# Up stage of two feed-forward blocks: block work of the head on VectorE alone, five gate tiles ahead

## The chip, the cores and the metric

The kernel runs on one core of a Trainium2 chip (trn2). The core has TensorE (PE in the profile, its weight loads PEld), VectorE (DVE), ScalarE (ACT), GpSimd (POOL) and SyncE (SP), which issues most of the transfers. Each engine runs its own list of instructions in order; semaphores tie the lists together. The metric is the device time of one execution in microseconds, the median of three runs: 2109.07 us for the kernel before.

## The reference

One layer of an encoder over 1040 rows (1024 and 16 meta rows) of 1024 features:

```python
h = h + 0.5 * swiglu(rmsnorm(h, ffn1_norm[l]), ffn1_w_gate[l], ffn1_w_up[l], ffn1_w_down[l])
u = rmsnorm(h, mix_norm[l]);  z = u @ w_in[l]
...  # differential attention (4 heads) and windowed attention (8 heads), both into w_out
h = h + jnp.concatenate([out_a, out_b], axis=-1) @ w_out[l]
h = h + 0.5 * swiglu(rmsnorm(h, ffn2_norm[l]), ffn2_w_gate[l], ffn2_w_up[l], ffn2_w_down[l])
h = rmsnorm(h, final_norm);  return h[:, N_META:]

def swiglu(x, w_gate, w_up, w_down):
    return (jax.nn.silu(x @ w_gate) * (x @ w_up)) @ w_down
```

The hidden width of a SwiGLU is 2816, that is 22 tiles of 128. All is float32. The change touches the normed input and the gate and up products of both SwiGLU blocks.

## The kernel before

**Stages.** In order: the up stage of the first SwiGLU (`ffn_up`, 1040 columns in two halves of H = 520), its down stage, the projections, both attentions, the output product, the up stage of the second SwiGLU (1024 columns, H = 512), its down stage and the last norm. A matrix product of float32 numbers is made of three passes: each operand is split into a rounded part (`hi`, a cast on ScalarE, line 117) and the rest (`lo`, a subtraction, line 114), and `product` (line 226) adds hi x hi, hi x lo and lo x hi.

**The up stage.** The normed input is cut in four blocks: feature half 1 or 2 by column half a or b. `b11` and `b21` are the two feature halves of column half a, `b22` the second feature half of column half b. Gate and up products of all 22 tiles are made by a Strassen-like scheme from seven block operands: `b11`, `b21`, `b22` and the differences `t1` to `t4`. Per tile there are seven products, each of four 128-row steps times three passes; where H is 520 each pass is two matmuls of 260 columns (24 matmuls a product), where H is 512 one (12 matmuls a product). Two of the seven (`lead_a` with `b11`, `lead_b` with `b21`) need column half a alone and can be made ahead of the rest; their weights go through tiles `rg0` (raw, two buffers), `wah` and `wal` (hi and lo, three buffers). The other five need `t2`, `t1`, `t3`, `b22` and `t4`, in that order in a tile, with weight sums `s1`, `s2`, `s4` made on GpSimd.

**The head.** "Head 1" is the start of the program, up to the point where products follow each other without a break; "head 2" is the same place in the second up stage. In it `prepare` loads or makes column halves a and b (tiles `ha`, `hc` and `hb`, `hd`) and norms half a (`first_half`, 16 pieces of work: norm, line 149, and split), and `combine` does half b (`second_half`): norms, differences, splits. `eng()` there deals the subtractions out to VectorE and GpSimd by prices of 0.61 and 1.24. `prepare1` sums the squares for the norm by additions on VectorE, `combine1` by additions on VectorE and GpSimd; a product with `ones` (line 650) sums over the partitions. Between the pieces of `second_half` four gate tiles (`LEAD = 4`) are interleaved, at its yields.

**The order of the work.** The program is written in this order, and a scheduler then places each instruction in the list of its engine by a timeline that it reckons; so an engine's list is not the order of the text. A list is kept on the chip: an instruction that waits holds up all behind it on its engine.

Of the kernel before, what the change touches and what calls it, by code (L numbers as in the profile page):

```python
# [34 lines left out]
OFF = 248  # L35
LEAD = 4
G_BUFS = 3
# [14 lines left out]
def layer(  # L52
# [137 lines left out]
    def ffn_up(H, wg, wu, nlead, prepare, combine, accs):  # L190
# [5 lines left out]
        with ExitStack() as st:  # L196
# [40 lines left out]

            ahead = {}

            def lead_a(f, src):  # L240
# [12 lines left out]

            def lead(f):
                def src(i):
                    t = la3.tile([P, hw], F32, tag="rg0", name="rg0", bufs=2)
                    nc.sync.dma_start(t, wg[f][:, i * hw : (i + 1) * hw])
                    return t

                lead_a(f, src)  # L260
                lead_b(f, src)

            with ExitStack() as st_r:
                lr = Rings(st_r, "lr", "right")
                for tag, bufs in (
                    ("nsq", 2), ("ns", 1), ("nr", 1), *((n, 1) for n in accs), ("ha", hk), ("hb", hk), ("x2", hk), ("hc", hk), ("hd", hk),
                ):
# [5 lines left out]
                la3 = Rings(st, "la3").reserve("rg0", 2).reserve("wah", 3).reserve("wal", 3)  # L273
# [8 lines left out]
            for tag, bufs in (  # L282
                ("rg0", 1), ("ru0", 1), ("s", 3), ("wbh", 2), ("wbl", 2), ("rg1", 1), ("ru1", 1),
                ("u2", 1), ("m5", 1), ("u3", 1), ("wch", 3), ("wcl", 3), ("ge", 1), ("gt", 1), ("g", G_BUFS),
            ):
                la4.reserve(tag, bufs)
# [9 lines left out]
            for f in range(FT):  # L296
# [6 lines left out]
                def s_tile():  # L303
                    return la4.tile([P, hw], F32, tag="s", name="s", bufs=3)
# [9 lines left out]
                product(p2, weight(la4, "wb", s2, 2), "t2", True)  # L314
                if nxt is not None:
# [4 lines left out]
                p3, p3f = ps_tile("p3")  # L320
                product(p3, weight(la4, "wb", s1, 2), "t1", True)
                tt(gp, a21, a11, a21, ALU.subtract)
# [14 lines left out]

                g2 = tmp(la5, "ge" if paired and not odd else "g", G_BUFS)
                tt(gp, u3, u3, m5, ALU.add)
# [16 lines left out]
                if not paired:  # L356
                    nc.gpsimd.dma_start(g_d[f][:, :H], g1)
                elif odd:
                    put("b21", g1)
                    tt(nc.vector, t2, g1, t2, ALU.subtract)  # L360
                    put("t4", t2)
                else:
                    put("b11", g1)
                    t1 = tmp(la5, "gt")
# [12 lines left out]
    def second_half(firsts, hts, gi, r, blk, pool, H):  # L377
        hk = KT // 2
        load = {nc.vector: 0.0, nc.gpsimd: 0.0}
        price = {nc.vector: 0.61, nc.gpsimd: 1.24}  # L380

        def eng():
            e = min(load, key=lambda e: load[e] + price[e])
            load[e] += price[e]
            return e

        def parts(n, j, src):
            hi, lo = (t[:, j, :] for t in blk[n])
            split(hi, lo, src, eng())

        x2 = {}
# [12 lines left out]
        yield  # L404
        for j in range(hk):
            tt(eng(), hts[j], hts[j + hk], hts[j], ALU.subtract)
            parts("t3", j, hts[j])
        for j in range(hk):
            parts("b22", j, hts[j + hk])
        for j in range(hk):  # L410
            b21 = firsts[j + hk]
            tt(eng(), b21, b21, x2[j], ALU.subtract)
            parts("t4", j, b21)

# [216 lines left out]

    E1, E2 = ([nc.vector if c == "v" else nc.gpsimd for c in e] for e in ("vv", "vp"))

    def rstd_pair(srcs, n, width, pool, subs, full, engs):

        half = len(srcs) // 2
        accs = []
        for c, eng in enumerate(engs):
            acc = pool.tile([P, 520], F32, tag=f"nacc{c}", name="nacc")[:, :n]
            for i, s in enumerate(srcs[c::2]):  # L640
                if i == 0:
                    nc.scalar.activation(acc, s, AF.Square)
                else:
                    sq = pool.tile([P, 520], F32, tag="nsq", name="nsq")[:, :n]
                    nc.scalar.activation(sq, s, AF.Square)
                    tt(eng, acc, acc, sq, ALU.add)
            accs.append(acc)
        for c, acc in enumerate(accs):
            for o, (c0, cn) in subs:
                nc.tensor.matmul(o, ones, acc[:, c0 : c0 + cn], start=c == 0, stop=c == len(accs) - 1)  # L650
        return newton(n, width, pool, full)

    def prepare1(pool, psum, blk, ps_tile, subs):
# [15 lines left out]
    def combine1(state, pool, blk, ps_tile, subs):  # L669
        H = L // 2  # L670
        a, b = state
        outs, full = ps_tile("p2")
        r = rstd_pair(b, H, D, pool, list(zip(outs, subs)), full, E2)
        yield
        yield from second_half(a, b, 0, r, blk, pool, H)
# [600 lines left out]
    def combine2(halves, pool, blk, ps_tile, subs):  # L1276
# [3 lines left out]
        r = rstd(b, H, D, pool, list(zip(outs, subs)), full)  # L1280
        yield
        yield from second_half(a, b, 2, r, blk, pool, H)
# [115 lines left out]
```

## Time and profile before

| what | value |
|---|---|
| median of 3 runs | 2109.07 us (2106.53 to 2112.87) |
| profiled execution, its own time | 2112.15 us |
| its span | 2110.4 us |
| PE busy | 1947.8 us, 92% of the span |
| PEld, DVE, ACT, POOL busy | 1695.8, 1304.6, 877.2, 1042.0 us |
| share of the chain that ended last: PE, DVE, DMA | 70%, 11%, 6% |

The profiled execution is 1.75 us longer than its span (work around the span), and 3.1 us above the median. TensorE is busy for most of the span; the chain that ended last runs over it. Where it is idle is read stage by stage. PEclk is the clock granted to TensorE, 1.00 for 2.4 GHz and 0.50 for 1.2 GHz.

### The profile page before, as it was taken

What the parts mean: (1) busy time and instruction counts of PE and PEld (TensorE: products, weight loads), DVE (VectorE), ACT (ScalarE), POOL (GpSimd) and SP (SyncE); (2) the same over time, 40 slices, a digit from 0 to 9 for tenths busy, and PEclk for the clock granted to TensorE, in tenths of its full rate; (3) what the DMA queues carried; (4) which work ended last, traced back from release to release, by engine and by line L of the source; (5) the groups of instructions that cost most, each with busy time, mean ns of one, the idle gap of its engine ahead of it and who ended that gap; (6) DMA issues with size and microseconds to landing.
All of it is one profiled execution on the core that took longest, in us unless ns stands there. A gap on an engine that the chain in (4) does not pass through costs nothing.

```text
span 2110.4 us, 30362 instructions
## 1 busy us (share of the span) xinstructions
PE 1947.8 (92%) x11484; PEld 1695.8 (80%) x11484; DVE 1304.6 (62%) x1804; ACT 877.2 (42%) x1609; POOL 1042.0 (49%) x856
## 2 busy tenths in 40 slices
PE   4799999998999999899977999877999999989998
PEld 4799999998999889777755777665788888867877
DVE  7865555547865572276667777478555555488745
ACT  5333333334532441266557666343333333344433
POOL 5655545444543651476457433036655545455453
PEclk9899999999999999999989999998999999999999
DMA  3232232327431452444442321522422332284222
GB/s 134 90 121 88 96 116 83 105 85 289 159 114 33 160 161 76 126 132 122 98 122 63 102 87 54 161 80 70 140 105 79 116 105 90 105 313 162 74 80 80
DMA packets 104563, 241.52 MB, mean 114 GB/s; under 512 B 14048, under 2 KB 28848, under 8 KB 104416
## 3 DMA queue, kind: packets, MB, share of 16 engines
q1 hardware_dynamic: 92896, 201.91, 30.3%
q0 software_dynamic: 11520, 37.67, 4.6%
q8 instruction: 90, 1.47, 0.3%
q14 instruction: 57, 0.47, 0.1%
HBM read 167.23 MB, written 65.44 MB: 110 GB/s over the span
## 4 chain that ended last, share of the span: by engine, by line
PE 70%; DVE 11%; DMA 6%; ACT 5%; POOL 3%; issue 3%; SPq 1%; DVEq 0%; POOLq 0%; ACTq 0%
PE p L226 37%; PE pA L557 8%; PE pC L557 4%; PE pj L167 4%; PE pv L867 3%; PE pd L167 2%; PE do L1166 2%; PE pB L557 2%; PE ds L763 2%; PE po L167 1%; DVE bl L114 1%; PE do L167 1%; PE wo L1000 1%; ACT dp L769 1%; PE wt L989 1%
## 5 line engine op out<-in xcount | busy, mean ns | idle before, releaser
L226 PE MATMUL p<-b_hi,wal 128*128 128x260 f32 (+1 forms) x528 | 146.5, 333 | 26.9 <-DVE wal L114 26.9
L226 PE MATMUL p<-b_hi,wah 128*128 128x260 f32 (+1 forms) x528 | 147.8, 334 | 13.2 <-ACT m L244 9.8
L226 PE MATMUL p<-b_lo,wah 128*128 128x260 f32 (+1 forms) x528 | 145.6, 331 | 7.7 <-DVE b_lo L114 7.7
L226 PE MATMUL p<-t_hi,wch 128*128 128x260 f32 (+1 forms) x528 | 140.5, 320 | 3.6 <-DVE u L114 3.6
L226 PE MATMUL p<-t_lo,wbh 128*128 128x260 f32 (+1 forms) x528 | 142.6, 320 | 0.0
L226 PE MATMUL p<-t_hi,wbh 128*128 128x260 f32 (+1 forms) x528 | 140.0, 321 | 1.5 <-ACT wbh L117 1.5
L226 PE MATMUL p<-t_lo,wch 128*128 128x260 f32 (+1 forms) x528 | 140.4, 320 | 0.0
L226 PE MATMUL p<-t_hi,wcl 128*128 128x260 f32 (+1 forms) x528 | 139.9, 319 | 0.0
L226 PE MATMUL p<-t_hi,wbl 128*128 128x260 f32 (+1 forms) x528 | 139.9, 320 | 0.0
L114 DVE TENSOR_TENSOR u<-p,m 128x520 f32<-128x520 f32 (+1 forms) x88 | 61.0, 693 | 111.2 <-PE p L226 107.4
L226 PEld LDWEIGHTS p<-b_hi,wal 128*128 128x128 f32 x528 | 92.2, 199 | 36.7 <-DVE wal L114 28.7
L117 ACT CAST wbh<-s 128x512 fp32r<-128x512 f32 x88 | 54.6, 621 | 156.2 <-PE p L226 149.4
L114 DVE TENSOR_TENSOR wal<-rg,wah 128x512 fp32r<-128x512 f32 x88 | 81.0, 922 | 61.9 <-ACT wah L117 61.8
L557 PE MATMUL pA<-bl,wh 128*128 128x260 f32 (+1 forms) x432 | 115.6, 322 | 1.6 <-DVE bl L114 1.6
L557 PE MATMUL pA<-bh,wh 128*128 128x260 f32 (+1 forms) x432 | 116.0, 323 | 1.0 <-DVE h L564 1.0
L114 DVE TENSOR_TENSOR bl<-r,bh 128x520 fp32r<-128x520 f32 (+1 forms) x126 | 111.3, 913 | 4.9 <-ACT bh L117 4.9
L117 ACT CAST wch<-ru 128x512 fp32r<-128x512 f32 x88 | 54.7, 622 | 143.4 <-PE p L226 72.9
L114 POOL TENSOR_TENSOR s<-ru 128x512 f32<-128x512 f32 x44 | 59.8, 1358 | 109.9 <-DVE wbl L114 90.7
L117 ACT CAST wah<-rg 128x512 fp32r<-128x512 f32 x88 | 54.1, 619 | 140.2 <-PE p L226 123.6
L557 PE MATMUL pA<-bh,wl 128*128 128x260 f32 (+1 forms) x432 | 112.2, 320 | 0.0
L226 PEld LDWEIGHTS p<-b_hi,wah 128*128 128x128 f32 x528 | 92.5, 199 | 24.1 <-ACT m L244 11.1
L564 DVE SCALAR_TENSOR_TENSOR h<-pA,h 128x520 f32<-128x520 f32 (+1 forms) x96 | 66.3, 692 | 68.1 <-PE pA L557 67.8
(288 smaller groups left out, 6099.1 us busy)
## 6 DMA issues: line engine op xcount, KB each, us to landing
rg<-wg SPq DMA_DIRECT2D x44, 512.0 KB, 3.6
ru<-wu SPq DMA_DIRECT2D x44, 512.0 KB, 5.3
wr<-wd SPq DMA_DIRECT2D x24, 768.0 KB, 4.4
r<-g_t SPq DMA_DIRECT2D x12, 780.0 KB, 6.0
r<-g_t SPq DMA_DIRECT2D x12, 768.0 KB, 5.8
g_b<-g POOLq DMA_DIRECT2D x27, 260.0 KB, 5.5
r<-g_b SPq DMA_DIRECT2D x9, 780.0 KB, 5.7
g_b<-g POOLq DMA_DIRECT2D x27, 256.0 KB, 5.3
```

The lines of the kernel that those rows point to most:

```text
L114: eng.tensor_tensor(out, a, b, op=op)
L117: nc.scalar.copy(hi, src)
L167: nc.tensor.matmul(o, w, x[:, c0 : c0 + n], start=first and i == 0, stop=last and i == 2)
L226: nc.tensor.matmul(o, w_k(ww, k), x[:, k, c0 : c0 + cn], start=first and k == 0 and i == 0, stop=k == hk - 1 and i == 2, skip_group_check= ...
L557: nc.tensor.matmul(o, w_k(ww, k), xx[:, c0 : c0 + cn], start=new and k == 0 and q == 0, stop=k == DNG - 1 and q == 2, skip_group_check=not ...
L564: nc.vector.scalar_tensor_tensor(hs, full, 0.5, hs, op0=ALU.mult, op1=ALU.add)
L763: nc.tensor.matmul(o, qs[c][:, qt * P : (qt + 1) * P], kk[:, c0 : c0 + n], start=i == 0, stop=i == 1)
L769: nc.scalar.activation(p, full, AF.Exp, bias=mx, scale=-1.0, accum_out=z[:, c : c + 1])
L867: nc.tensor.matmul(ps[:m, 192 + c * 320 : 512 + c * 320], u[:, k, sl], w[:, k, c * 320 : (c + 1) * 320], start=k == 0 and i == 0, stop=k = ...
L989: nc.tensor.transpose(pt[:m, g * P : (g + 1) * P], p4[:, g, c0 : c0 + m], ident)
L1000: nc.tensor.matmul(po, vb[:m, vt, kv, :], t[:m, :], start=j == 1 and i == 0, stop=j == nk + 1 and i == 1)
L1166: nc.tensor.matmul(po[:, :256], v[:m, j, :], at[:m, j, :], start=j == 0, stop=j == NB)
```

## The change

- All work on the blocks is on VectorE: the splits of half a, and all subtractions and splits of half b. `eng()`, its prices and the list of engines for the squares go.
- `t4`'s difference is formed as soon as its `x2` is there, so two buffers of `x2` do in place of four.
- Five gate tiles are made ahead in place of four (`LEAD = 5`); three of their ten half products are written ahead of `combine`, the others at its yields.
- The first tile's sums `s1` and `s2` are made on VectorE from three early half loads (`first_sums`) and split ahead, through `wah` and `wal`, in place of two sums on GpSimd and a split through `wbh` and `wbl`.
- In head 1 the squares of half a are summed on TensorE (`rstd_each`: each square goes into the product with `ones`), not by additions on VectorE; those of half b by additions on VectorE alone.
- Tiles `s` move to a pool that opens earlier; `ge` and `gt` go, and `rg0` serves in their place once the head is done.

```diff
-LEAD = 4
+LEAD = 5
...
+            def first_sums():
+                a22, a21, a11 = part(wu, 0, 1, "s", 3), part(wu, 0, 0, "s", 3), part(wg, 0, 0, "s", 3)
+                tt(nc.vector, a22, a21, a22, ALU.add)
+                tt(nc.vector, a11, a22, a11, ALU.subtract)
+                first.update(s1=a22, s2=a11)
+
+            def early_work():
+                for f in range(nlead):
+                    for i, step in enumerate((lead_a, lead_b)):
+                        if f == nlead - 1 and i == 1:
+                            first_sums()
+                        step(f, lambda i: part(wg, f, i))
+                        yield
+                for n in ("s2", "s1"):
+                    first["w" + n] = weight(la3, "wa", first[n], 3)
+                    yield
...
-                nl = 0
-                for _ in combine(state, lr, blk, ps_tile, subs):
-                    if nl < nlead:
-                        lead(nl)
-                        nl += 1
+                early = early_work()
+                for _ in range(3):
+                    next(early)
+                for n in combine(state, lr, blk, ps_tile, subs):
+                    for _ in range(n):
+                        next(early, None)
+                for _ in early:
+                    pass
...
-                s1, s2, s4 = s_tile(), s_tile(), s_tile()
                 gp = nc.gpsimd
-                tt(gp, s1, a21, a22, ALU.add)
-                tt(gp, s2, s1, a11, ALU.subtract)
+                if f:
+                    s1, s2 = s_tile(), s_tile()
+                    tt(gp, s1, a21, a22, ALU.add)
+                    tt(gp, s2, s1, a11, ALU.subtract)
+                else:
+                    s1, s2 = first["s1"], first["s2"]
...
-            split(hi[:, k % hk, :], lo[:, k % hk, :], hts[k], nc.vector if k < hk else nc.gpsimd)
+            split(hi[:, k % hk, :], lo[:, k % hk, :], hts[k])
...
         for j in range(hk):
-            b11, b12, b22 = firsts[j], hts[j], hts[j + hk]
+            b11, b21, b12, b22 = firsts[j], firsts[j + hk], hts[j], hts[j + hk]
             normed(b12, b12, gi, j, r)
             normed(b22, b22, gi, j + hk, r)
-            load[nc.vector] += 1.34
-            x2[j] = pool.tile([P, H], F32, tag="x2", name="x2", bufs=4)
-            tt(eng(), b11, b12, b11, ALU.subtract)
-            tt(eng(), x2[j], b22, b11, ALU.subtract)
-            parts("t2", j, x2[j])
-            yield
+            less(b11, b12, b11)
+            x2 = pool.tile([P, H], F32, tag="x2", name="x2", bufs=2)
+            less(x2, b22, b11)
+            parts("t2", j, x2)
+            less(b21, b21, x2)
+            yield 2 if j == hk - 1 else 1
...
+    def rstd_each(srcs, n, width, pool, subs, full):
+
+        for i, s in enumerate(srcs):
+            sq = pool.tile([P, 520], F32, tag="nsq", name="nsq")[:, :n]
+            nc.scalar.activation(sq, s, AF.Square)
+            for o, (c0, cn) in subs:
+                nc.tensor.matmul(o, ones, sq[:, c0 : c0 + cn], start=i == 0, stop=i == len(srcs) - 1)
         return newton(n, width, pool, full)
...
-        r = rstd_pair(a, H, D, pool, list(zip(outs, subs)), full, E1)
+        r = rstd_each(a, H, D, pool, list(zip(outs, subs)), full)
...
-        yield
+        yield 2
         yield from second_half(a, b, 2, r, blk, pool, H)
```

How the lists move, at three places.

GpSimd, the first sums of squares and blocks of head 1. Before, its list begins with the squares (`nacc`), then parts of blocks (`b_lo`, `t_lo`) and differences (`ha`, `hb`, `hc`, `x`):

```order
L114 TENSOR_TENSOR nacc<-nacc,nsq 128x520 x3
L114 TENSOR_TENSOR b_lo<-hc,b_hi 128x520 x4
L114 TENSOR_TENSOR ha<-hb,ha 128x520 x4
L114 TENSOR_TENSOR x_631<-hd,ha 128x520
L114 TENSOR_TENSOR hb<-hd,hb 128x520
L114 TENSOR_TENSOR b_lo<-hd,b_hi 128x520
L114 TENSOR_TENSOR t_lo<-ha,t_hi 128x520
L114 TENSOR_TENSOR hc<-hc,x_631 128x520
L114 TENSOR_TENSOR s<-ru 128x512
L114 TENSOR_TENSOR t_lo<-x_487,t_hi 128x520
```

Now it begins with what the tiles' weights need (`ru`, `s`), and no block stands in it:

```order
L114 TENSOR_TENSOR ru<-rg,ru 128x512
L114 TENSOR_TENSOR s<-ru 128x512
L114 TENSOR_TENSOR s<-rg,s 128x512
L114 TENSOR_TENSOR ru<-rg,ru 128x512
L114 TENSOR_TENSOR s<-s,rg 128x512
L114 TENSOR_TENSOR s<-rg,s 128x512
```

All block work has left this list.

VectorE, the last blocks of head 1 ahead of the weights of the first tile's other products. `rg_` with a number is the raw weight of a gate half; `wal<-s` is the first tile's early split. Before, the fourth tile's gate halves are still to come when the blocks end:

```order
L114 TENSOR_TENSOR hc<-hc,x_487 128x520
L114 TENSOR_TENSOR b_lo<-hd,b_hi 128x520
L114 TENSOR_TENSOR wal<-rg_565,wah 128x512
L114 TENSOR_TENSOR t_lo<-ha,t_hi 128x520
L114 TENSOR_TENSOR hc<-hc,x_559 128x520
L114 TENSOR_TENSOR t_lo<-x_631,t_hi 128x520
L114 TENSOR_TENSOR t_lo<-x_559,t_hi 128x520
L114 TENSOR_TENSOR t_lo<-hb,t_hi 128x520
L114 TENSOR_TENSOR hc<-hc,x_703 128x520
L114 TENSOR_TENSOR wal<-rg_597,wah 128x512
L114 TENSOR_TENSOR t_lo<-hb,t_hi 128x520
L114 TENSOR_TENSOR t_lo<-hc,t_hi 128x520 x2
```

Now the fifth tile's (`rg_728` and `rg_768`) stand among the last blocks, and the first tile's two splits right behind:

```order
L114 TENSOR_TENSOR x_682<-hd,ha 128x520
L114 TENSOR_TENSOR x_722<-hd,ha 128x520
L114 TENSOR_TENSOR t_lo<-hc,t_hi 128x520
L114 TENSOR_TENSOR wal<-rg_728,wah 128x512
L114 TENSOR_TENSOR hc<-hc,x_682 128x520
L114 TENSOR_TENSOR wal<-rg_768,wah 128x512
L114 TENSOR_TENSOR hc<-hc,x_722 128x520
L114 TENSOR_TENSOR t_lo<-x_682,t_hi 128x520
L114 TENSOR_TENSOR t_lo<-x_722,t_hi 128x520
L114 TENSOR_TENSOR wal<-s,wah 128x512
L114 TENSOR_TENSOR t_lo<-hc,t_hi 128x520 x2
L114 TENSOR_TENSOR wal<-s,wah 128x512
```

The two gate halves of a fifth tile have come in between the blocks, and the splits of the first tile's own sums stand at the end.

ScalarE, head 2, around the norm of half b (`nr`, line 139). Before, the norm comes first and then the table of the SiLU is loaded once:

```order
L139 ACTIVATE nr<-p_15649,eps 128x512
L140 ACTIVATE ns<-nr 128x512
L117 CAST wah<-rg_15797 128x512
L117 CAST wah<-rg_15777 128x512
L251 ACT_TABLE_LOAD
L251 ACTIVATE sg<-p_15680 128x512
```

Now two SiLUs (`sg`) of early tiles come ahead of the norm, with a table load for each change:

```order
L252 ACT_TABLE_LOAD
L252 ACTIVATE sg<-p_15664 128x512
L252 ACTIVATE sg<-p_15705 128x512
L117 CAST wah<-rg_15835 128x512
L139 ACT_TABLE_LOAD
L139 ACTIVATE nr<-p_15726,eps 128x512
L140 ACTIVATE ns<-nr 128x512
```

The norm has moved behind two SiLUs, a weight cast and two table loads; a third load follows when the next SiLU comes.

## Rows read from the trace of the kernel before

**Rows 1.** Busy us (x instructions): PE, PEld, DVE, ACT, POOL; PEclk, DMA share
```profile
26.50:76.00 49.50, 24.36 (x137) 23.48 (x137) 49.43 (x42) 21.45 (x37) 37.96 (x23) 0.79 0.13 41
1413.00:1451.00 38.00, 18.70 (x52) 12.51 (x51) 38.00 (x34) 17.15 (x29) 28.47 (x17) 0.73 0.11 32
```

**Rows 2.** Waits of TensorE from 26 to 80 us: total, times, longest
```profile
PE p L226 <- DVE wal L114: 17.4, 2, 14.2
PE p L226 <- DVE b_lo L114: 5.5, 1, 5.5
```

**Rows 3.** VectorE in order of time, head 1: start, us, engine, line, operation
```profile
18.80 0.70 DVE L142 SCALAR_TENSOR_TENSOR nr<-ns,nr 128x520 f32<-128x520 f32 x1
...
36.90 0.76 DVE L149 SCALAR_TENSOR_TENSOR hb<-hb,gains,nr 128x520 f32<-128x520 f32 x1
37.58 0.76 DVE L149 SCALAR_TENSOR_TENSOR hd<-hd,gains,nr 128x520 f32<-128x520 f32 x1
...
53.97 1.78 DVE L114 TENSOR_TENSOR hb<-hd,hb 128x520 f32<-128x520 f32 x1
...
60.75 0.69 DVE L114 TENSOR_TENSOR x<-hd,ha 128x520 f32<-128x520 f32 x1
61.35 0.69 DVE L114 TENSOR_TENSOR hb<-hd,hb 128x520 f32<-128x520 f32 x1
...
74.10 3.50 DVE L114 TENSOR_TENSOR t_lo<-hc,t_hi 128x520 fp32r<-128x520 f32 x2
```

**Rows 4.** GpSimd in order of time, the same stretch
```profile
53.46 1.74 POOL L114 TENSOR_TENSOR hc<-hc,x 128x520 f32<-128x520 f32 x1
...
62.17 1.62 POOL L114 TENSOR_TENSOR t_lo<-x,t_hi 128x520 fp32r<-128x520 f32 x1 [1.90 <-ACT t_hi L117]
```

**Rows 5.** Line 226 by stretch: PE, PEld busy (x matmuls), PEclk, DMA
```profile
0.00:80.00 80.00, 30.10 (x163) 28.65 (x164) 0.85 0.32 108
80.00:90.00 10.00, 10.00 (x86) 10.00 (x85) 1.00 0.43 156
1398.00:1460.00 62.00, 37.82 (x122) 27.08 (x122) 0.81 0.21 70
1460.00:1470.00 10.00, 9.78 (x42) 7.92 (x43) 1.00 0.27 97
```

**Rows 6.** TensorE in order of time, head 1
```profile
11.49 4.24 PE L650 MATMUL p<-nacc,ones 128*128 128x260 f32 x8 [11.49 <-DVE nacc L114]
...
32.05 0.80 PE L226 MATMUL p<-b_lo,wah 128*128 128x260 f32 x2 [5.49 <-DVE b_lo L114]
...
37.76 0.40 PE L226 MATMUL p<-b_hi,wal 128*128 128x260 f32 x2
```

**Rows 7.** ScalarE in order of time, head 1
```profile
3.51 1.37 ACT L642 ACTIVATE nacc<-ha 128x520 f32<-128x520 f32 x2 [1.28 <-DMA ha<-hT]
...
10.79 1.32 ACT L645 ACTIVATE nsq<-hc 128x520 f32<-128x520 f32 x2 [0.24 <-DVE nacc L114]
...
15.76 0.69 ACT L139 ACTIVATE nr<-p,eps 128x520 f32<-128x520 f32 x1
...
24.12 0.61 ACT L117 CAST wah<-rg 128x512 fp32r<-128x512 f32 x1
...
46.71 1.28 ACT L251 ACT_TABLE_LOAD   x1
```

**Rows 8.** Transfers issued from 1340 to 1465 us: KB each, median us to landing
```profile
rg<-wg SPq DMA_DIRECT2D x7, 256.0 KB, 3.1
```

**Rows 9.** VectorE in order of time, head 2
```profile
1404.70 0.68 DVE L114 TENSOR_TENSOR hd<-po,hd 128x512 f32<-128x512 f32 x1
...
1410.90 0.69 DVE L142 SCALAR_TENSOR_TENSOR nr<-ns,nr 128x512 f32<-128x512 f32 x1
```

**Rows 10.** Busy time in a stretch ahead of head 2, columns of rows 1
```profile
1350.00:1360.00 10.00, 7.04 (x27) 4.82 (x26) 4.42 (x8) 3.05 (x5) 0.00 (x0) 0.93 0.63 180
```

**Rows 11.** Waits of the transfer queue from 0 to 95 us: total, times, longest
```profile
SPq L257 <- DVE wal L114: 43.0, 6, 18.4
```

More of the change, by code (lines that the diff above doesn't have):

```diff
@@ L238, in ffn_up @@
             ahead = {}
+            first = {}
             def lead_a(f, src):
@@ L252, in lead_b, with part @@
                 ahead[f] = [m1, sg]
[L254 to L261, printed above, removed]
+            def part(w, f, i, tag="rg0", bufs=2):
+                t = la3.tile([P, max(hw, H)], F32, tag=tag, name=tag, bufs=bufs)[:, :hw]
+                nc.sync.dma_start(t, w[f][:, i * hw : (i + 1) * hw])
+                return t
+            def first_sums():
[13 more added lines that the diff above has]
+                    yield
             with ExitStack() as st_r:
@@ L303, in s_tile @@
                 def s_tile():
-                    return la4.tile([P, hw], F32, tag="s", name="s", bufs=3)
+                    return la3.tile([P, max(hw, H)], F32, tag="s", name="s", bufs=3)[:, :hw]
                 def src(i):
                     return raws[nxt][:, i * hw : (i + 1) * hw]
-                s1, s2, s4 = s_tile(), s_tile(), s_tile()
                 gp = nc.gpsimd
-                tt(gp, s1, a21, a22, ALU.add)
-                tt(gp, s2, s1, a11, ALU.subtract)
+                if f:
[4 more added lines that the diff above has]
+                    s1, s2 = first["s1"], first["s2"]
+                s4 = s_tile()
                 p2, p2f = ps_tile("p2")
-                product(p2, weight(la4, "wb", s2, 2), "t2", True)
+                product(p2, weight(la4, "wb", s2, 2) if f else first["ws2"], "t2", True)
                 if nxt is not None:
@@ L320, in ffn_up @@
                 p3, p3f = ps_tile("p3")
-                product(p3, weight(la4, "wb", s1, 2), "t1", True)
+                product(p3, weight(la4, "wb", s1, 2) if f else first["ws1"], "t1", True)
                 tt(gp, a21, a11, a21, ALU.subtract)
@@ L336, in put @@
                     nc.gpsimd.dma_start(g_b[pair // DNG][n][pair % DNG][:, :H], t)
-                g2 = tmp(la5, "ge" if paired and not odd else "g", G_BUFS)
+                g2 = tmp(la3, "rg0", 2) if paired and not odd else tmp(la5, "g", G_BUFS)
                 tt(gp, u3, u3, m5, ALU.add)
@@ L363, in ffn_up @@
                     put("b11", g1)
-                    t1 = tmp(la5, "gt")
+                    t1 = tmp(la3, "rg0", 2)
                     tt(nc.vector, t1, g2, g1, ALU.subtract)
@@ L378, in second_half, with less @@
         hk = KT // 2
[L379 to L385, printed above, removed]
         def parts(n, j, src):
             hi, lo = (t[:, j, :] for t in blk[n])
[L389 to L391 removed]
+            split(hi, lo, src)
+        def less(out, a, b):
+            tt(nc.vector, out, a, b, ALU.subtract)
         for j in range(hk):
[L393 removed]
+            b11, b21, b12, b22 = firsts[j], firsts[j + hk], hts[j], hts[j + hk]
             normed(b12, b12, gi, j, r)
             normed(b22, b22, gi, j + hk, r)
[L396 to L401 removed]
+            less(b11, b12, b11)
[4 more added lines that the diff above has]
+            yield 2 if j == hk - 1 else 1
         for j in range(hk):
             parts("t1", j, firsts[j])
[L404 removed]
+            yield j % 2
         for j in range(hk):
[L406 removed]
+            less(hts[j], hts[j + hk], hts[j])
             parts("t3", j, hts[j])
+            yield 1
         for j in range(hk):
@@ L410, in second_half @@
         for j in range(hk):
-            b21 = firsts[j + hk]
-            tt(eng(), b21, b21, x2[j], ALU.subtract)
-            parts("t4", j, b21)
+            parts("t4", j, firsts[j + hk])
     def down_strassen(h, wd, T, load_h):
@@ L629, in down_last, with rstd_pair @@
             pass
-    E1, E2 = ([nc.vector if c == "v" else nc.gpsimd for c in e] for e in ("vv", "vp"))
-    def rstd_pair(srcs, n, width, pool, subs, full, engs):
-        half = len(srcs) // 2
+    def rstd_pair(srcs, n, width, pool, subs, full):
         accs = []
-        for c, eng in enumerate(engs):
+        for c in range(2):
             acc = pool.tile([P, 520], F32, tag=f"nacc{c}", name="nacc")[:, :n]
@@ L645, in rstd_pair @@
                     nc.scalar.activation(sq, s, AF.Square)
-                    tt(eng, acc, acc, sq, ALU.add)
+                    tt(nc.vector, acc, acc, sq, ALU.add)
             accs.append(acc)
@@ L672, in combine1 @@
         outs, full = ps_tile("p2")
-        r = rstd_pair(b, H, D, pool, list(zip(outs, subs)), full, E2)
-        yield
+        r = rstd_pair(b, H, D, pool, list(zip(outs, subs)), full)
+        yield 2
         yield from second_half(a, b, 0, r, blk, pool, H)
```

11 lines of the change are left out of this document (6 added, 5 removed).

## Prediction

> **What bounds the kernel now.** I read the page's shares first: TensorE is busy 92% of the span and carries 70% of the chain that ended last, so only its idle stretches and slow stretches can give time back. The table of windows then shows where these are: the head of each up stage. From 26.5 to 76 us TensorE is busy 24.36 of 49.5 us and from 1413 to 1451 us 18.70 of 38, at a mean granted clock of 0.79 and 0.73 of 2.4 GHz, while VectorE is busy without a break [rows 1]. In the waits of TensorE the reader is to see who ends the idle time: `wal`, the low part of a gate weight, 17.4 us in two waits, and `b_lo`, 5.5 us [rows 2]. Both are VectorE instructions that waited for nothing but their turn. So each head is set by VectorE's list, and two things make that list long.
>
> The first is how long an instruction takes. With GpSimd idle the subtractions of 520 columns start 0.60 us apart (60.75, 61.35) and norms 0.68 apart (36.90, 37.58); with GpSimd running beside them one takes 1.78 (53.97) in place of 0.69 [rows 3]; the GpSimd instruction takes 1.74 there [rows 4]. So each GpSimd instruction costs VectorE about 1.09 us. The windows bear this out: 42 x 0.60 + 23 x 1.09 = 50.3 us against 49.43 measured, and 34 x 0.60 + 17 x 1.09 = 38.9 against 38.00 [rows 1]. Dealing an instruction to GpSimd saves VectorE 0.60 and costs it 1.09.
>
> The second is the order: TensorE had early gate work to do and waited 14.2 us in one piece for its weight, which stood behind block work [rows 2].
>
> **How the gain is counted.** I compare when TensorE has done the same number of products. Head 1: after the change ten gate halves are made early, with 24 matmuls each, and eight matmuls of the first tile's `t2` and `t1` stand ahead of the last half: 248. Before, line 226 has done 163 by 80.0 us and then 86 in 10 us without a break, so 248 at 80 + 85/8.6 = 89.9 us [rows 5]. Head 2, with 12 matmuls a product: ten halves, `t2` and `t1`, 144; before, 122 by 1460 and 42 in the next 10 us, so 144 at 1465.2 [rows 5]. Behind these points products follow each other in both kernels and the total of products is the same, so the difference of these times is the gain.
>
> **Head 1, step by step.**
> - *Opening sum.* Before, four matmuls with `ones` take 4.24 us and end at 15.73 [rows 6]; the norm factor `nr` is there at 19.50 [rows 3], 3.8 later. Now there are 16 of them (8 squares, two column chunks), and six additions are off VectorE. At 4.24/4 = 1.06 each they take 17.0 us. They can start when the first square is done, 3.51 + 1.37/2 = 4.2 [rows 7], and so end at 21.2 at the latest. The earliest end follows from the squares: the last of half a is done at 10.79 + 1.32 = 12.1 [rows 7], plus one pair, 14.2. I take 18, since the matmuls run one behind the other from the first square on and the clock should rise on the way: after the starts at 32.05 it took 5.7 us until two matmuls read 0.40 for 0.80 [rows 6]. `nr` then comes at 21.8, 2.3 later than now.
> - *What moves to VectorE.* From `nr` to the last gate weight part (`wal<-rg_768` in the lists above) VectorE has 70 instructions: 16 norms; two steps of the norm of half b, two additions of squares, two weight sums, nine weight parts, eight low parts of `b11` and `b21`, four of `b22`, four each of the differences into `ha` and `hb` and of `x2`, three into `hc`, and low parts of `t1` (4), `t2` (2), `t3` (4), `t4` (2), which is 54. That is 16 x 0.68 + 54 x 0.60 = 43.3 us. GpSimd now holds only weight sums in its list; I let two fall into this stretch, 2.2 us. End: 21.8 + 45.5 = 67.3.
> - *Casts and loads under it.* A block's cast takes ScalarE 0.61 [rows 7], no more than VectorE's step beside it. Each gate half is loaded into the buffer of the one before last, so its load begins when that one's weight part is done. In the new list most lie eight or more VectorE instructions apart, 5 us, and load (3.1 us, rows of head 2 [rows 8]), cast and hand-over need about 4.3. I charge nothing in head 1; without that cover it is up to 4.3 us for each.
> - *TensorE.* After that last weight part it needs one gate half, 24 x 0.116 = 2.8 us: 70.1. Gaps of a few us remain ahead of it, and after a gap the clock falls, so I add 2: 72.1.
>
> Gain in head 1: 89.9 - 72.1 = 17.8 us. Ends: opening sum at 14.2 (+3.8), no GpSimd in the way (+2.2), no slow clock (+2): 25.8. Opening sum at 21.2 (-3.2), five more GpSimd instructions (-5.5), 3 us more of slow clock: 6.1.
>
> **Head 2.** Half a is ready under the output product, as now, and the `b_lo` parts no longer wait for GpSimd. But the norm of half b comes later than its 1411.6 of now [rows 9]. Four gate weight parts now stand ahead of it in VectorE's list, in two rounds, each beginning with a load that may start only when the round before is done: from the last addition into `hd` (1405.4 [rows 9]) two rounds of 3.1 + 0.61 + 0.60 give 1414, the full-size weight load in the same queue adds about 1, and on ScalarE a table load (1.28), the two steps of the norm (0.69 the first, the second like a cast, 0.61; all [rows 7]) and two VectorE steps follow: 1419. From there 47 instructions to the last low part of `t2`, 8 x 0.68 + 39 x 0.60 = 28.8, and two of GpSimd, 2.2: 1450. The rest of `t2` takes 1.4, and the next weight stands behind the addition that reads `t2`, 1.0: 1452.4. Gain: 1465.2 - 1452.4 = 12.8.
>
> The order has two more table loads than before, 2 x 1.28; only the one ahead of the norm is on the path. The Trainium skill ("ScalarE: Activation LUTs", "Table sets: the hidden batching unit") speaks against this order: group functions by table set, since each change costs a load, which it puts at about 2.7 us. Here a load took 1.28 us [rows 7]; by the page's figure the gain in head 2 would be 1.4 less, and the total as much later.
>
> Four more half weight loads (1 MB) fall under the output product, where the transfers are busy 0.63 of the time at 180 GB/s [rows 10]: 5 us of transfers if nothing hides them, nothing if all is hidden. I charge 1. Gain in head 2: 11.8. Ends: no rounds of loads ahead of the norm (+7.4), none for transfers and weight (+2): 21. Five more GpSimd instructions (-5.5), all of the transfers (-4): 2.3.
>
> Tiles that share `rg0` in place of `ge` and `gt` have as many buffers as before, and nothing else in the tile loop changes: 0, or a us either way.
>
> **Sum.** 17.8 + 11.8 = 29.6 us. The profiled execution took 2112.15, so 2082.6; the median is 3.1 lower, so 2079.5 by that. I say 2081. The ends of both heads give 8.4 to 46.8, that is 2064 to 2103.
>
> **Rivals.**
> - *VectorE stands for early weights.* Its list is now strict and short, and each wait for a gate half stops all blocks behind it. For it: before, the transfer queue waited six times for `wal`, 18.4 us the longest, so the ring of two buffers is tight [rows 11], and the two rounds in head 2. Against: the spacing in head 1. Four such stops of 4.3 us beyond my sum leave 12 us: 2098.
> - *Both heads go to their upper end.* The sums run at full clock behind the squares and the loads of head 2 are there in time: 41 us, 2070. The Trainium skill ("TensorE: Matmul & The Clock Gate", "Part 1: The HAM clock gate") says that a TensorE kept busy goes to its full clock; by this the second half of the opening sums would run twice as fast and they would end about 2 us before my 18. In this trace the four sums, 4.24 us without a break, stayed at the slow pace, so it isn't shown for them.
> - *No change that can be told,* within 0.3% or 6.3 us: eight stops of the first kind, with the rest as forecast.
> - *Slower.* The long VectorE instructions are not GpSimd's doing but the stretch's (transfers, casts and matmuls on the same tiles), and stay at 49.43/42 = 1.18 us. Then the 70 + 47 instructions, 45.5 and 31 us in my sum, take 82.6 and 55.5: head 1 ends 37 later, head 2 24 later, and the time is 2081 + 61 = 2142. It decides from a mean of 0.65 + 29.6/117 = 0.90 us on. Against it: the two instructions at 60.75 and 61.35 ran in the same stretch at 0.69, just while GpSimd paused until 62.17 [rows 3, 4]. For it: at 74.10 two took 3.50 with GpSimd in one instruction for part of that [rows 3].
>
> **How the numbers follow.** The sum 0.66 (own range 2072 to 2090), early weights 0.17 (2091 to 2103), upper end 0.07, no change 0.05, slower 0.05. From 2068 to 2097 lie all of the first, over half of the second and most of the third, some 0.8. Faster by over 0.3%: 0.66 + 0.17 + 0.07 = 0.90; the same 0.05, slower 0.05.
>
> **What would show it.** In the profile after: VectorE instructions of 520 columns at 0.69 from about 22 to 67 us, and no GpSimd block work; `nr` of head 1 near 22; the last early `wal` near 67; 248 matmuls of the up stage by 72; no wait of TensorE above 5 us from 34 us on. In head 2 the norm of half b near 1419 less head 1's gain, and 144 matmuls 13 us sooner in the stage. It is wrong if VectorE is idle ahead of weight parts for more than 5 us in a head, if instructions stay over 0.9, or if the stages behind the heads differ by more than 2 us.

## The result, and the profile after

| kernel | median of its runs | profiled execution, its span |
|---|---|---|
| before (runs beside it) | 2110.97 us (4 runs) | 2112.15, 2110.4 |
| changed | 2088.07 us (2085.49 to 2091.47, 4 runs) | 2091.47, 2089.7 |

The ratio is 0.9893, 95% interval 0.9866 to 0.9921: faster by 22.9 us, in the profiled executions by 20.7. I had forecast 2081 us, a gain of 29.6, with a range of 2068 to 2097.

**Where the gain arose.** Each tile has one copy of `p` into `m5` on ScalarE (line 324 before, 346 after). That of the eleventh tile lies far behind a head, where products follow each other. Before, in both up stages:

```profile
276.68 0.59 ACT L324 COPY m<-p 128x520 f32<-128x520 f32 x1
...
1642.43 0.58 ACT L324 COPY m<-p 128x512 f32<-128x512 f32 x1
```

After:

```profile
259.72 0.59 ACT L346 COPY m<-p 128x520 f32<-128x520 f32 x1
...
1619.66 0.58 ACT L346 COPY m<-p 128x512 f32<-128x512 f32 x1
```

So the lead is 17.0 us behind head 1 (forecast 17.8) and 22.8 behind head 2. The first early product of head 2 started at 1398.34 before and at 1381.44 after, a lead of 16.9, so head 2 itself gave 5.9, and not 11.8.

**Head 1 and VectorE.** The windows that answer to [rows 1]; head 2's is laid 17 us earlier, as the head is. Columns as there:

```profile
26.50:76.00 49.50, 41.29 (x285) 39.87 (x286) 47.59 (x72) 29.21 (x50) 10.04 (x5) 0.85 0.26 86
1396.00:1434.00 38.00, 25.02 (x89) 17.50 (x88) 31.64 (x52) 23.41 (x40) 26.48 (x2) 0.92 0.12 40
```

In head 1 VectorE did 72 instructions in 47.59 us, 0.66 each, where 42 took 49.43. TensorE did 285 matmuls in place of 137. Its waits from 26 to 80 us, against [rows 2]:

```profile
PE p L664 <- DVE nacc L114: 4.6, 1, 4.6
PE p L226 <- DVE wal L114: 4.4, 2, 2.7
PE p L226 <- DVE u L114: 1.3, 1, 1.3
```

**Head 2 and GpSimd.** The row that I had not foreseen is in GpSimd's list. Its rows in the two heads, up to the end of the blocks:

```profile
36.30 1.29 POOL L114 TENSOR_TENSOR ru<-rg,ru 128x512 f32<-128x512 f32 x1 [32.17 <-DMA ru<-wu]
...
67.25 4.14 POOL L114 TENSOR_TENSOR s<-ru 128x512 f32<-128x512 f32 x1 [29.66 <-DMA ru<-wu]
...
1404.94 25.25 POOL L114 TENSOR_TENSOR ru<-rg,ru 128x512 f32<-128x512 f32 x1 [74.00 <-DVE hb L149]
1430.15 1.27 POOL L114 TENSOR_TENSOR s<-rg,s 128x512 f32<-128x512 f32 x1
```

The difference a11 - a21 of the first tile (`ru<-rg,ru`) took 25.25 us; alone such an instruction takes about 1.3 (the row below it). VectorE in the same stretch, at the norm, and around its first idle time:

```profile
1400.19 0.69 DVE L142 SCALAR_TENSOR_TENSOR nr<-ns,nr 128x512 f32<-128x512 f32 x1
...
1404.71 0.75 DVE L149 SCALAR_TENSOR_TENSOR hd<-hd,gains,nr 128x512 f32<-128x512 f32 x1
1405.38 0.75 DVE L149 SCALAR_TENSOR_TENSOR hb<-hb,gains,nr 128x512 f32<-128x512 f32 x1
...
1428.38 0.69 DVE L114 TENSOR_TENSOR hc<-hc,x 128x512 f32<-128x512 f32 x1
1432.63 0.69 DVE L114 TENSOR_TENSOR t_lo<-x,t_hi 128x512 fp32r<-128x512 f32 x1 [3.56 <-ACT t_hi L117]
```

VectorE's instructions start 0.60 to 0.67 us apart and none is lengthened. It goes idle at 1428.38 + 0.69 = 1429.07, and GpSimd's ends 1.1 us later. In head 1, 67.25 + 4.14 = 71.39 lies 1.15 behind VectorE's idle time from 70.24 on. So the instruction did not run slowly: it did not start until VectorE paused. Who hung on it is read from ScalarE, and from the transfer queue's and TensorE's waits:

```profile
1425.49 0.62 ACT L117 CAST t_hi<-x 128x512 fp32r<-128x512 f32 x1 [2.99 <-DVE x L114]
1430.22 0.62 ACT L117 CAST wch<-ru 128x512 fp32r<-128x512 f32 x1 [4.11 <-POOL ru L114]
1430.75 0.58 ACT L346 COPY m<-p 128x512 f32<-128x512 f32 x1
1431.46 0.62 ACT L117 CAST wch<-s 128x512 fp32r<-128x512 f32 x1
1431.98 0.61 ACT L117 CAST t_hi<-x 128x512 fp32r<-128x512 f32 x1
```

```profile
SPq L311 <- POOL s L114: 35.3, 2, 29.5
```

```profile
PE p L226 <- ACT wch L117: 5.5, 1, 5.5
PE p L226 <- DVE wal L114: 2.8, 2, 1.9
PE p L226 <- ACT wbh L117: 2.6, 1, 2.6
```

The cast `wch<-ru` stood in ScalarE's list ahead of the cast `t_hi<-x`, on which one of VectorE's last `t_lo` waited; the loads for the second tile could leave only when GpSimd had read the first tile's raw weight. TensorE waited 5.5 us for `wch`, ahead of its 140th matmul of the stage, and 2.6 for `wbh` of the second tile, ahead of the 149th. Behind the long wait the granted clock was 0.50 (1.2 GHz), and from 1432 to 1444 TensorE did 18 matmuls. The stretch in which it made the 145th to the 240th matmul, after and before, shows the difference (columns as in [rows 1]):

```profile
1432.00:1444.00 12.00, 8.45 (x18) 5.75 (x19) 7.15 (x9) 3.50 (x7) 5.76 (x4) 0.50 0.51 176
1434.00:1463.80 29.80, 26.37 (x98) 19.80 (x97) 17.25 (x22) 7.93 (x13) 19.25 (x15) 0.82 0.37 126
```

```profile
1465.20:1487.60 22.40, 22.40 (x97) 18.05 (x96) 14.28 (x18) 7.72 (x13) 13.98 (x12) 1.00 0.21 71
```

Of the 7.4 us that it took longer, 3.4 were waits (`wbh` 2.6, `u` 0.8); the other 4.0 go with the lower clock, at which the matmuls start 0.43 us apart in place of 0.23, up to 1444.6.

### The profile page after: what moved, and what is told of

It reads as the page before. It is cut to its first block, busy times and chain, and to the rows that moved or that the text cites. A ratio compares the mean times of both kernels' runs of the same rounds, so it can differ in the third digit from the quotient of the medians.

```text
span 2089.7 us, 30414 instructions
## 1 busy us (share of the span) xinstructions
PE 1956.9 (94%) x11508; PEld 1701.2 (81%) x11508; DVE 1262.0 (60%) x1843; ACT 882.8 (42%) x1611; POOL 993.3 (48%) x811
## 5 line engine op out<-in xcount | busy, mean ns | idle before, releaser
L226 PE MATMUL p<-b_hi,wal 128*128 128x260 f32 (+1 forms) x528 | 142.3, 325 | 6.4 <-DVE wal L114 6.4
L114 POOL TENSOR_TENSOR ru<-rg,ru 128x512 f32<-128x512 f32 x44 | 87.6, 1990 | 106.8 <-DVE hb L149 74.0
L226 PE MATMUL p<-t_hi,wbh 128*128 128x260 f32 (+1 forms) x504 | 133.7, 321 | 2.6 <-ACT wbh L117 2.6
L226 PE MATMUL p<-t_lo,wbh 128*128 128x260 f32 (+1 forms) x504 | 135.9, 320 | 0.0
L226 PE MATMUL p<-t_hi,wbl 128*128 128x260 f32 (+1 forms) x504 | 133.3, 320 | 0.0
L114 POOL TENSOR_TENSOR s<-wr 128x384 f32<-128x384 f32 x48 | 55.2, 1153 | 114.0 <-DVE wl L114 94.2
L117 ACT CAST wh<-s 128x384 fp32r<-128x384 f32 x96 | 49.1, 515 | 136.8 <-PE pA L574 66.6
```

The lines of the kernel that those rows point to most:

```text
L114: eng.tensor_tensor(out, a, b, op=op)
L117: nc.scalar.copy(hi, src)
L226: nc.tensor.matmul(o, w_k(ww, k), x[:, k, c0 : c0 + cn], start=first and k == 0 and i == 0, stop=k == hk - 1 and i == 2, skip_group_check= ...
```

## The experiments

E1 to E8 take up one part each; E9 to E11 ran side by side. "Own" is head 2's own gain: the lead at the eleventh tile's copy less the lead at the first early product, all against the profiled execution of before, worked out as above. Medians of before beside them were 2109.07 to 2110.97.

| kernel | lead behind head 1 | at the start of head 2 | behind head 2 | own | median, us |
|---|---|---|---|---|---|
| changed | 17.0 | 16.9 | 22.8 | 5.9 | 2088.07 |
| E1 first tile on VectorE | 17.2 | 16.9 | 30.6 | 13.8 | 2085.18 |
| E2 before, blocks on VectorE | 8.7 | 10.6 | 16.1 | 5.5 | 2095.61 |
| E3 blocks dealt | 3.3 | 4.9 | 9.0 | 4.1 | 2102.30 |
| E4 probe | 17.1 | 17.2 | 29.1 | 11.9 | 2081.20 (2 runs) |
| E5 four gate tiles | 12.2 | 16.5 | 24.3 | 7.8 | 2094.59 |
| E6 opening sum by additions | 18.8 | 21.5 | 28.0 | 6.6 | 2088.56 |
| E7 first sums on GpSimd | 15.6 | 18.4 | 27.4 | 9.0 | 2087.76 |
| E8 probe by releaser | 15.2 | 11.8 | 20.8 | 9.1 | 2092.77 (2 runs) |
| E9 changed again | 17.0 | 14.2 | 20.8 | 6.6 | 2092.22 |
| E10 = E1 again | 18.6 | 24.3 | 38.1 | 13.8 | 2083.52 |
| E11 E1 and E6 | 17.5 | 16.0 | 26.9 | 10.9 | 2088.28 |

The second column of leads less the first shows what the stages between the heads add, at which no edit is aimed: from -3.4 to +5.7 us, and for one and the same kernel -0.3 (E1) and +5.7 (E10). So a single time tells little under 6 us, while head 2's own gain came out alike for the kernels that ran twice (5.9 and 6.6, 13.8 and 13.8) and in E6, whose head 2 is the changed kernel's (6.6). E4 and E11, whose head 2 is made as in E1 (but for E4's three small instructions), gave 11.9 and 10.9: up to 192 matmuls they keep E1's pace (63.0 and 64.0 us from the first early product, E1 64.3), and the next 48 take 14.8 us in place of 11.7; in E11's lists the order of the second tile's weights differs there.

**E1, the first tile's GpSimd work on VectorE.**

```diff
-                tt(gp, a21, a11, a21, ALU.subtract)
+                tt(gp if f else nc.vector, a21, a11, a21, ALU.subtract)
...
-                tt(gp, s4, a12, s2, ALU.subtract)
+                tt(gp if f else nc.vector, s4, a12, s2, ALU.subtract)
```

> The changed kernel, with the first tile's two GpSimd instructions (the difference a11 - a21 and the sum s4) on VectorE as well, so that GpSimd has nothing to do while the blocks are made. Theory: in head 2 the GpSimd instruction that took 25.25 us did not get its turn until VectorE ran out of work, and ScalarE's list (a wch cast standing ahead of a t_hi cast) and the transfer queue (the next gate load waits for s4) hung on it. Then VectorE's 3.56 us of idle time near the end of the blocks goes, the loads for the second tile leave before the blocks end, and the products run without a break some 8 to 14 us sooner in head 2: 2074 to 2081 us. Rival: the end of the blocks and the norm of half b set head 2 anyway, and the long instruction lay beside: 2086 to 2091 us. Head 1 stays within 2 us either way.

2085.18 us, ratio to before 0.9880 (0.9865 to 0.9894). The time fell between the two theories; the stage did not: head 2's own gain is 13.8 in place of 5.9, so having GpSimd's two instructions there cost 7.9 us in this pair of executions (7.2 between E9 and E10). VectorE's list of E1, where the difference now is an instruction like any other and the idle time is gone:

```profile
1407.35 0.69 DVE L114 TENSOR_TENSOR ru<-rg,ru 128x512 f32<-128x512 f32 x1
...
1429.61 0.71 DVE L114 TENSOR_TENSOR hc<-hc,x 128x512 f32<-128x512 f32 x1
1430.21 0.71 DVE L114 TENSOR_TENSOR t_lo<-x,t_hi 128x512 fp32r<-128x512 f32 x1
```

**E2, the kernel before with block work on VectorE alone.** `eng()` gives VectorE always, the splits of `b21` and the squares of half b go to VectorE.

> The kernel before, with one thing changed: eng() always gives VectorE, the splits of b21 and the squares of half b are on VectorE too. Order, four gate tiles and GpSimd's weight sums stay. Theory (each GpSimd instruction beside VectorE costs it 1.09 us and saves it 0.60): head 1 has some 20 such instructions less and head 2 some 15, so VectorE's lists shorten by about 10 and 7 us; gate weights still stand behind blocks, and the weight sums that GpSimd keeps may be held until VectorE pauses, so I expect 2094 to 2104 us. Rival (the long instructions are the stretch's own): the lists grow by 20 x 1.18 and 15 x 1.18, 2140 us or more. Rival (order is all): 2108 to 2114 us.

2095.61 us, ratio 0.9927 (0.9914 to 0.9940), as the first theory said: taking GpSimd out of VectorE's way gives 14.4 us by itself, against 22.9 for the whole change, and half of head 1's gain (8.7 of 17.0). The window of head 1 shows 65 VectorE instructions at 0.63 each:

```profile
26.50:76.00 49.50, 31.76 (x203) 30.54 (x204) 40.75 (x65) 23.89 (x43) 24.12 (x7) 0.79 0.22 75
```

The first of the weight sums left on GpSimd was held in both heads:

```profile
43.52 16.18 POOL L114 TENSOR_TENSOR s<-ru 128x512 f32<-128x512 f32 x1 [39.39 <-DVE b_lo L114]
...
1415.00 15.52 POOL L114 TENSOR_TENSOR s<-ru 128x512 f32<-128x512 f32 x1 [76.88 <-DVE ha L114]
```

**E3, the blocks of half b dealt out again**, by the prices of before, in the changed kernel's order.

```diff
-            split(hi, lo, src)
+            split(hi, lo, src, eng())
...
-            tt(nc.vector, out, a, b, ALU.subtract)
+            tt(eng(), out, a, b, ALU.subtract)
```

> The changed kernel, with the subtractions and splits of half b dealt out to VectorE and GpSimd by the prices of the kernel before (0.61 and 1.24). Theory (a GpSimd instruction costs VectorE 1.09 us): some 12 instructions of each head move, each a net loss of 0.48, so 6 us a head, and more where products wait for a block that GpSimd has not done: 2094 to 2106 us. If a lone GpSimd instruction is held until VectorE pauses, blocks on GpSimd come late and it is the upper end or more. Rival (the long instructions are not GpSimd's doing): VectorE's list is shorter by 12 x 0.60 in each head, 2074 to 2082 us.

2102.30 us, ratio 0.9966 (0.9953 to 0.9980), with 49.33 us for 52 VectorE instructions in the window of head 1, 0.95 each:

```profile
26.50:76.00 49.50, 33.06 (x203) 31.23 (x204) 49.33 (x52) 25.80 (x44) 29.31 (x17) 0.76 0.22 71
```

The prediction's prices hold: 52 x 0.60 + 17 x 1.09 = 49.7 us. The rival "the long instructions are not GpSimd's doing" is out by E2 and E3 together. E3 also tells what the new order, the opening sum and the fifth tile give in head 1 while GpSimd still does blocks of half b: 3.3 us. With four tiles and all blocks on VectorE, E5 less E2 (12.2 less 8.7) leaves 3.5 us for the order, the opening sum and the first tile's sums, which no run timed apart.

**E4 and E8, small instructions on GpSimd.** E4 has three (256, 64, 64 columns) beside the norms of half b, E8 eight of 64 columns among line 114's subtractions.

> The kernel of e1 with three small GpSimd subtractions in each head (256, 64 and 64 columns into a scratch tile that nobody reads), which may start when the first norm of half b's second feature half is done on VectorE, early in its stretch without a break. Theory (GpSimd's instruction with two inputs waits until VectorE's list pauses): the first takes 15 to 35 us, whatever its size, and ends about when VectorE first is idle; the time is that of e1 within 3 us, since nobody waits for them. Rival (they take turns, as the records of the kernel before read): each ends within 1.5 us and one VectorE instruction for each is longer by up to 0.6 us. Rival (size sets it): the first takes half of a 512 column one, 0.6 us alone, and nothing on VectorE changes.

E4's theory failed: the three took turns. (Its time, 4.0 us below E1's, lies a little outside the 3 us expected; it is of two runs.) GpSimd, and VectorE's norm beside the first, 1.11 us in place of 0.76:

```profile
40.06 2.48 POOL L114 TENSOR_TENSOR pr<-hd 128x256 f32<-128x256 f32 x3 [35.94 <-DVE hd L149]
```

```profile
39.89 0.76 DVE L149 SCALAR_TENSOR_TENSOR hb<-hb,gains,nr 128x520 f32<-128x520 f32 x1
40.56 1.11 DVE L149 SCALAR_TENSOR_TENSOR hd<-hd,gains,nr 128x520 f32<-128x520 f32 x1
```

> The kernel of e1 with eight GpSimd subtractions of 64 columns in each head, into scratch tiles that nobody reads: four may start when VectorE has made a piece of the t4 difference, four when ScalarE has cast a piece of t2. All fall among the subtractions of line 114. In e4 the three small ones, released by a norm on VectorE, took turns at once (2.48 and 2.39 us for three), while the instructions released by a transfer were held until VectorE was idle (4.5 us), in the same run. Theory A (only the releaser matters: what VectorE or ScalarE releases gets in at the next boundary of VectorE's list, what a transfer releases doesn't): all sixteen end within 1.2 us. Theory B (what matters is the stretch: among norms GpSimd gets in, among line 114's subtractions it doesn't unless VectorE has a gap): several are held, 3 to 20 us. The time is that of e1 within 5 us.

Theory B of E8 held. Of eight in a head the first did not get in until VectorE paused, and most of the others ran behind it at 0.27 us each (the first row of each head holds two of them: the first ended 18.29 and 16.28 us after its start). GpSimd:

```profile
50.73 18.54 POOL L114 TENSOR_TENSOR pr<-t_hi 128x64 f32<-128x64 f32 x2 [46.62 <-ACT t_hi L117]
69.23 0.54 POOL L114 TENSOR_TENSOR pr<-hc 128x64 f32<-128x64 f32 x2
...
1419.81 16.53 POOL L114 TENSOR_TENSOR pr<-t_hi 128x64 f32<-128x64 f32 x2 [83.79 <-ACT t_hi L117]
```

VectorE, whose first pause in head 1 began at 68.18 + 0.68 = 68.86:

```profile
68.18 0.68 DVE L114 TENSOR_TENSOR t_lo<-x,t_hi 128x520 fp32r<-128x520 f32 x1
70.98 1.32 DVE L114 TENSOR_TENSOR t_lo<-hc,t_hi 128x520 fp32r<-128x520 f32 x1 [2.12 <-ACT t_hi L117]
```

So a small size does not keep an instruction from being held, nor does a releaser other than a transfer: 64 columns, released by ScalarE, waited 18 us. The time did not keep to what was expected: 2092.77 us is 7.6 above E1, not within 5 (two runs). Head 2 shows how a held instruction can cost time even when nobody reads its result. ScalarE's cast `wch<-ru` waited for it, though the difference in `ru` had been made on VectorE long before (that it waited to reuse a buffer is likely, but not shown), and TensorE waited for the cast, 4.8 us against 1.2 in E1:

```profile
1436.62 0.62 ACT L117 CAST wch<-ru 128x512 fp32r<-128x512 f32 x1 [4.13 <-POOL pr L114]
```

```profile
PE p L226 <- ACT wch L117: 4.8, 1, 4.8
```

**E5, four gate tiles (LEAD = 4).**

> The changed kernel with four early gate tiles in place of five (LEAD = 4). Theory (the fifth tile fills TensorE's time while VectorE makes blocks): its two gate halves are 48 matmuls in head 1 and 24 in head 2, 5.6 us each at full clock, which then are made later; VectorE has two weight parts less in each head, 1.2 us. So the second tile's products come 4 us later in each head, 2088 to 2098 us. Rival (VectorE's list alone sets the end of a head, and early work beyond it only lengthens the list): 2084 to 2088 us.

2094.59 us, ratio 0.9939 (0.9917 to 0.9961). Behind head 1 the lead is 12.2, so the fifth tile is worth 4.8 us there, as the first theory had it. In head 2 nothing was held this time (the two GpSimd instructions took 1.85 and 1.65 us), so its 7.8 is to be set beside E1's 13.8: 6.0, with the turns of these two instructions in it, since E1 has none on GpSimd there.

**E6, the opening sum by additions** (`rstd_pair` in place of `rstd_each` in `prepare1`).

> The changed kernel, with the squares of half a summed by additions on VectorE and four products with ones, as before, in place of sixteen. The trace after has the norm factor nr 1.7 us later than before (21.17 against 19.50). Theory (nr starts VectorE's stretch, and all of head 1 hangs on it): head 1 is 1 to 2 us shorter, 2086 to 2088 us. Rival (the sixteen products bring TensorE's clock up for the first gate products): 2089 to 2092 us. Rival: VectorE slow in its additions gives nr the same time, no change.

2088.56 us, ratio 0.9901 (0.9883 to 0.9919), no different from the changed kernel. Behind head 1 it leads by 1.8 us more, but E10 beside E1 shows 1.4 us between two executions of one kernel there. Whether the sixteen products pay stays open.

**E7, the first tile's sums on GpSimd** (`first_sums` and its two early splits left out).

> The changed kernel without the early sums of the first tile: s1 and s2 are made on GpSimd and split through wbh and wbl, as in every later tile. VectorE has two sums less; its two splits come behind the blocks. Theory (a GpSimd instruction that comes into VectorE's stretch is held until it ends, as the 25.25 us one was): in head 2 three GpSimd instructions in place of one are held or done behind the blocks, and the first tile's t2 waits for sum, difference, cast and split, 1.3 + 1.3 + 0.6 + 0.7 us behind the blocks: the second tile of head 2 comes 4 to 8 us later than in the changed kernel; in head 1, where its load lands ahead of the stretch's last third, 0 to 4 us: 2092 to 2100 us. Rival (GpSimd gets its turn and the sums lie beside the blocks): 2086 to 2090 us.

2087.76 us, ratio 0.9901 (0.9880 to 0.9921): the rival was right. GpSimd got in at the norms and did four instructions in turns with VectorE, a21's difference among them, and nothing hung on a held one. Head 2's own gain is 9.0 all the same, and not E1's 13.8; four turns at the 1.09 us of [rows 3] would be 4.4 of that, by estimate:

```profile
1402.93 1.36 POOL L114 TENSOR_TENSOR s<-ru 128x512 f32<-128x512 f32 x1 [74.17 <-DMA ru<-wu]
1404.37 1.59 POOL L114 TENSOR_TENSOR s<-s,rg 128x512 f32<-128x512 f32 x1
1405.92 1.72 POOL L114 TENSOR_TENSOR ru<-rg,ru 128x512 f32<-128x512 f32 x1
1407.61 1.73 POOL L114 TENSOR_TENSOR s<-rg,s 128x512 f32<-128x512 f32 x1
```

**E9 to E11, side by side.** E9 is the changed kernel, E10 is E1, E11 is E1 with E6's edit.

> The changed kernel itself, unaltered, beside the next two, so that the three stand on one chip. It has run at 2088 us; the long GpSimd instruction of head 2 should be there again if it is no accident of one execution: 15 to 26 us, ending about 1.1 us after VectorE's first idle time. Rival (an accident): 1.2 to 2 us, and the second tile of head 2 some 8 us sooner.

> The kernel of e1 again (the first tile's difference and s4 on VectorE), beside the changed kernel. By the stages, e1 was 8 us ahead of the changed kernel behind head 2, but its median only 3 us lower. Theory (the 8 us are real, and what lies between is run to run spread of the stages behind): 4 to 9 us below e9. Rival (the stages behind give it back): within 3 us of e9.

> e1 with the opening sum of squares by additions on VectorE, as in the kernel before. Each part alone stood well: e6 was 1.8 us ahead of the changed kernel behind head 1, e1 8 us behind head 2. If they add up: 6 to 11 us below e9, 2077 to 2082 us. Rival (a block more in VectorE's list ahead of the norm of half b, or a load that VectorE now waits for, takes it back): within 3 us of e10.

E9: 2092.22 us, ratio 0.9923 (0.9903 to 0.9943). It is neither the theory nor the rival to the letter: the difference got in, and the next instruction, `s4`, was held, 7.69 us, until 1433.69, 1.15 behind VectorE's pause from 1432.54. ScalarE's cast `wch<-s` hung on it, and head 2's own gain is 6.6, near the 5.9 of the first execution. (E6's head 2 went the same way, with 1.78 us for the difference and 7.71 for `s4`.) E9's two rows:

```profile
1407.28 1.77 POOL L114 TENSOR_TENSOR ru<-rg,ru 128x512 f32<-128x512 f32 x1 [73.74 <-DVE hb L149]
1426.00 7.69 POOL L114 TENSOR_TENSOR s<-rg,s 128x512 f32<-128x512 f32 x1 [16.95 <-DVE wal L114]
```

E10: 2083.52 us, ratio 0.9871 (0.9849 to 0.9893), 8.7 below E9 on the same chip; head 2's own gain is 13.8 again. So the first theory holds, and E10 is the version that beats both kernels. E11: 2088.28 us, ratio 0.9895 (0.9875 to 0.9916), 3.9 below E9 and 4.8 above E10, as neither theory had it; the two edits did not add up.

## Why the prediction was right, and where it was not

- *Bound and mechanism: right.* Both heads hung on VectorE's list, and GpSimd beside it was what made that list long (E2: 14.4 us by this alone; E3: dealing half b out again costs 14).
- *Opening sum: 2 us too long, of no effect.* It ended at 15.95, not 18, since the products got faster on the way: they start 0.43 us apart up to 10.68 and 0.22 apart from 11.08. These are the 2 us that the rival "Both heads go to their upper end" had counted on (by its own figures, 4.2 + 8.5 + 4.3 = 17.0, it would be one). The profile gives the granted clock as 1.00 in both parts, so it doesn't show that this was the clock. They took 10.61 us for 32 records, against 4.24 for 8 [rows 6]:

```profile
5.34 10.61 PE L673 MATMUL p<-nsq,ones 128*128 128x260 f32 x32 [5.34 <-DMA ones<-ones]
```

  `nr` was there at 21.2 all the same (forecast 21.8), as squares on ScalarE and other VectorE work stood ahead of it.
- *VectorE's list in head 1: right.* Last early weight part at 66.0 (forecast 67.3), 248 matmuls at 71.5 (72.1). Of that lead of 18.6 us, 1.6 went behind the point, at one wait of TensorE for `u` (1.3 us, in the rows above).
- *Norm of half b: right.* It ended at 1400.9, which with the lead of 16.9 is 1417.8 on the clock of before; 1419 was forecast, with about 1 us for a full-size weight load that was taken from no row. VectorE waited 7.6 us in three pieces for gate weights, the two load rounds. I had also named over 5 us of such idle time as a sign against me; by that sentence it is one, though the sum held these rounds.
- *Head 2 behind the blocks: wrong, and the reason for the miss.* The step that failed is the one under "How the gain is counted": "Behind these points products follow each other in both kernels". Up to 144 matmuls head 2 kept to the sum, though the wait for `wch` lies ahead of the 140th: they were done at 1434.0, 14.3 us sooner in the stage (12.8 forecast). The next 96 did not follow each other. They took 29.8 us in place of 22.4: 3.4 us of waits, and 4.0 at the clock that was still 0.50 from the wait for `wch`, a cost that the sum has in head 1 and puts at nothing here. The root is a term that I had charged on the wrong engine: "two of GpSimd, 2.2 us" of VectorE's time. VectorE paid nothing in this execution (in E9, where the difference took its turn, one norm took 1.78 us in place of 0.75); GpSimd's own instruction was held up to 25.25 us, and behind it stood ScalarE's list and the loads of the second tile. E1 takes it away, and head 2's own gain is 13.8 us, above the forecast of 11.8. E1 too loses on the way: its lead in the stage is 18.0 us at 144 matmuls (1430.34) and 13.8 at the eleventh tile, so the forecast there was right only as a sum: more was gained ahead of the point, and some lost behind it.
- *Tile loop: right.* From the eleventh to the last tile the lead stays within 0.3 us in the second up stage and falls from 17.0 to 16.1 in the first. The stages behind took 2.1 us back in the profiled execution (22.8 to 20.7), just over the 2 us that I had named as a sign against me; TensorE's 5.5 us for `wch` is over the 5 us that I had named, too.
- *Transfers, 1 us, and table loads:* not resolved; the stages between the heads vary by more.
- *Rivals.* "Early weights" took place in head 2 only as far as the sum had it. "Slower" is refuted (0.66 us an instruction, and E2). The upper end of head 2 (21) was not reached even in E1. The lower ends, 8.4 us, give 2102 us and not the 2103 of the sum; nothing rests on it.

The Trainium skill ("SBUF — State Buffer", "SBUF: two separate sides") says that VectorE and GpSimd share a pair of ports, that of a VectorE instruction with two inputs in SBUF and a GpSimd instruction that reads SBUF the one that starts first has the pair to its end, and that the other blocks fully. E4's pair of rows agrees for one instruction (1.11 us in place of 0.76). The section "A bandwidth-pool intuition that's wrong (but worth ruling out)" says, of GpSimd's descriptor writing, that the blocked one starts about when VectorE's instruction ends; here the 25.25 us instruction waited for 39 of them, and the measurement decides.

## What to carry to other kernels

When an engine is packed without gaps, look for single instructions of the engine that shares its path: what they cost may be not their length but the time until the packed engine pauses, and that cost falls on whoever waits for them. Give such lone instructions to the packed engine itself (8.7 us here, E10 against E9); to bring them ahead of the stretch would be another way, which no run here tried. And count a gain at a point behind which you have checked that the next weights are there too, and that no wait ahead of it has left TensorE at the lower clock.

## What the runs showed that I had not expected

A GpSimd subtraction beside VectorE's back-to-back subtractions has two fates: it takes turns, about 1.7 us each, or is held until VectorE pauses (25.25, 18.3, 16.3, 16.18, 15.52, 7.7 us), even when it has only 64 columns and runs in 0.27. Once one is in and others follow at once, they go on in turns. Which fate it meets was not settled: the same instruction of the same kernel, released by a norm both times, took 25.25 us in one execution and 1.77 in another, and neither its size, nor its releaser, nor norms against subtractions as neighbours separates all cases.
